# Attention in a two-layer diffusion backbone: the value products of two heads issued key block by key block in turns

## The chip, the cores and the metric

The kernel runs on one core of a Trainium2 chip. The metric is device time in microseconds (us) of one execution. A core has TensorE (PE, with its weight loads shown as PEld), VectorE (DVE), ScalarE (ACT), GpSimd (POOL), SyncE (SP) and 16 DMA engines. Each engine works through its own instructions in a fixed order and waits on semaphores for the others.

## The reference, cut to what matters

Two layers are computed over 512 latent tokens and 256 context tokens of 1024 features. Each layer projects its input, runs four token mixers (multi-head latent attention, an RWKV-7 scan, grouped-query attention, windowed grouped-query attention), merges them with gates, applies an output projection and a norm, then a product-key expert network and a second norm. The change touches the three attentions. Each has 8 heads with values of 64 features. For a block of 128 queries of one head:

```python
s = einsum('bqkgd,blkd->bkgql', q, k) * scale     # scores of 128 queries against n keys
p = softmax(s)                                     # a sink logit joins in windowed attention
o = einsum('bkgql,blkd->bqkgd', p, v)              # values weighted: n keys x 64 features
```

A latent query sees all 768 keys in the first two attentions, so 6 key blocks of 128. In windowed attention it sees 512 or 640 keys (4 or 5 blocks). A context query sees the 256 context keys (2 blocks). The last layer has no context queries.

## The kernel before, in words

Layer 0 and layer 1 go through the same stages: projections, RWKV scan, attention and merge, output projection and norm, experts, second norm. In the attention stage `branch` (line 1104) is called three times, for latent (L1203), grouped-query and windowed attention (both L1227). It goes over the head pairs `hp`, over the streams (latent and context), over the 128-query blocks `b` and over the two heads of the pair. For each of these it calls `attend` (line 1061), which

- multiplies queries and keys into the scores `S`, a PSUM tile called `pw` with two buffers (L1070; masks L1073),
- takes the row maximum on VectorE (L1075) and its scaled negative (L1077, with a sink L1079),
- takes the exponential with its row sum on ScalarE into `pp`, three buffers (L1081),
- takes the reciprocal (L1085) and normalises the row (L1086), both on VectorE,
- transposes `pp` block by block on TensorE (L182) into PSUM tiles `ptp`, four blocks to a tile, two buffers; a tile of four blocks is copied to `pt` by ScalarE (L1097), a shorter one by VectorE (L1095),
- multiplies the values by `pt`, one matmul for each key block, accumulated in the PSUM tile `po` (L1101). The stationary operand is 128 keys x 64 features, the moving one 128 keys x 128 queries. The first head of the pair writes partitions 0 to 63 of `po`, the second 64 to 127. `po` has one buffer; when all query blocks of a stream are done it is split into two parts by ScalarE and VectorE (L1127, L1128).

Operands of the value products are float32, and the trace has two records of MATMUL and two of LDWEIGHTS for each such product.

`merge` (line 1034) multiplies a finished branch by its output weights (matmuls into `pm`, L176), with two VectorE operations for each piece (L1049, L1051) and a split of each weight tile (L204, L205). The merge of the branch before is written behind each branch and runs in between the matmuls of the next one.

The attention stage has no order written out by hand. When the program is built, a planner of the framework puts each engine's instructions in a fixed order: it goes through its own estimate of the run, and whenever an engine is free it takes the ready instruction that was written first. So work written later fills in where earlier work isn't ready by its estimate, and the chip then follows that order whatever the true times are.

The lines that decide on the value products are these:

```python
kbs = [k0 // P + j for c0, k0, kn in ranges for j in range(kn // P)]
r0 = (h % 2) * 64
for j, kb in enumerate(kbs):
    pe.matmul(o[r0:r0 + 64, o0:o0 + P], vx(kb), pt[:, j * P:(j + 1) * P],
              start=(j == 0), stop=(j == nk - 1))
```

Of the kernel before, what the change touches and what calls it, by code (L numbers as in the profile page):

```python
# [8 lines left out]
F32 = mybir.dt.float32  # L9
# [9 lines left out]
P = 128  # L19
D = 1024  # L20
DC = 8
TL = 512
TC = 256
T = TL + TC
# [54 lines left out]
def tile_backbone(ctx: ExitStack, tc: tile.TileContext, I, out, taps=None, upto=99):  # L79
# [89 lines left out]
    def mm_acc(outs, lhs, rhs, nk):  # L169
        """outs: list of (psum ap, lo, hi); lhs/rhs: functions k -> (H, L); moving sliced by lo:hi"""  # L170
# [13 lines left out]
    # ------------------------------------------------------------------ weight stream  # L184
# [26 lines left out]
    # ------------------------------------------------------------------ modulation  # L211
# [3 lines left out]
    def ada_round(l, r, ps, sb, ring=None, bufs=4):  # L215
        """columns r * 2048 .. of layer l: four groups of 512, one column tile of the array each"""
# [30 lines left out]
    def xtiles(l):  # L247
        """the modulated input of layer l in two parts, latent and context, on the other side of SBUF"""
# [7 lines left out]
    # ------------------------------------------------------------------ layers  # L256
    for l in range(DEPTH):
# [5 lines left out]
        with xlat:  # L263
            # ---------------------------------------------------------- S1 projections
            T3B = 12
            with xctx, ExitStack() as e1:
# [42 lines left out]
                # RWKV features, transposed  # L309
                with ExitStack() as er:  # L310
# [76 lines left out]
                    def prepare(hp, r, k, v, kk, rt):  # L387
                        """decayed queries and keys of a pair of heads, bonus"""
# [95 lines left out]
                # natural projections  # L484
# [22 lines left out]
                def rope(dst, x, b, nh, hd):  # L507
                    """dst, x: [P, nh, hd]"""
# [80 lines left out]
                # context gates  # L589
# [36 lines left out]
            # ---------------------------------------------------------- S2 RWKV scan, latent gates  # L626
            ybscr = dram.tile([P, 4, T], F32, name=f"ybscr{l}")
            with ExitStack() as e2:
# [29 lines left out]
                class Halves:  # L658
                    """twelve chunks in two tiles: forward in the order of the steps, backward by chunk"""
# [9 lines left out]
                    def load(self, rows, src, first):  # L669
                        """src(a, b): chunks a .. b - 1"""  # L670
# [22 lines left out]
                def rwkv_pair(hp, loaded, others):  # L693
                    """others: what is left to do for the pair before, done between the parts of this one; yields
                    when only the norm is left"""
# [5 lines left out]
                    # Gram blocks  # L701
# [13 lines left out]
                    # inverse of the 32 x 32 diagonal blocks  # L715
# [7 lines left out]
                    # strictly causal part of the values, per step  # L723
# [59 lines left out]
                    # chunk recurrence  # L783
# [91 lines left out]
                    # group norm, bonus, gate  # L875
# [69 lines left out]
        def fold(pool, go, bo, m, kshift, kscale):  # L945
            """gain and bias of the norm, then scale and shift of the modulation, as one gain and one bias"""
# [8 lines left out]
        def layer_norm(pool, psv, pm, z, lo, hi, go, bo, dst, GB=None, dests=None, nat=None):  # L955
            """tokens lo..hi of z: [P, DC, TN], normalised in place over the features; pm: its column sums;
            dst: where the result goes; dests(lo, hi, s): where its modulated form goes, in two parts"""
# [57 lines left out]
        with ExitStack() as ep:  # L1015
# [7 lines left out]
            # -------------------------------------------------------------- S3 attention and merge  # L1023
            with ExitStack() as e3:
# [36 lines left out]
                def attend(pool, q, kx, vx, scale, h, o, o0, ranges, masks, sink):  # L1061
                    """one 128-query block of one head; ranges: (S column, first key, keys)"""
# [24 lines left out]
                    pt = pool.tile([P, T], F32, name=nm("pt"), tag="pt", bufs=3)  # L1087
# [10 lines left out]
                    kbs = [k0 // P + j for c0, k0, kn in ranges for j in range(kn // P)]  # L1098
                    r0 = (h % 2) * 64
                    for j, kb in enumerate(kbs):  # L1100
                        pe.matmul(o[r0:r0 + 64, o0:o0 + P], vx(kb), pt[:, j * P:(j + 1) * P],  # L1101
                                  start=(j == 0), stop=(j == nk - 1))
# [143 lines left out]
            with ExitStack() as eh:  # L1246
# [67 lines left out]
                def spend(e, c):  # L1314
                    """engine e is busy for c more"""
                    clock[e] = max(clock[e], clock["pe"] - SLACK[l]) + c
# [664 lines left out]
```

## Time and profile before

| what | value |
|---|---|
| time, median of 3 runs | 6534.53 us (6518.1 to 6548.82) |
| span of the profiled execution | 6533.5 us |
| PE busy | 5912.4 us (90%) |
| PEld busy | 4895.5 us (75%) |
| DVE busy | 4508.9 us (69%) |
| ACT busy | 2371.0 us (36%) |
| POOL busy | 2217.2 us (34%) |
| value products (L1101) in the chain that ended last | 4% of the span |

The span goes from the first to the last instruction of the profiled execution. Its own time isn't listed apart from the three timed runs; the span is 1.0 us under their median. Busy time is what an engine's records cover. Matmuls are pipelined and the ends of their records are modelled, so a row's time is longer than the step from one matmul to the next. "idle before it" is time in which an engine stood still ahead of an instruction, with the instruction whose end let it go.

### The profile page before, as it was taken

What the parts mean: (1) busy time and instruction counts of PE and PEld (TensorE: products, weight loads), DVE (VectorE), ACT (ScalarE), POOL (GpSimd) and SP (SyncE); (2) the same over time, 40 slices, a digit from 0 to 9 for tenths busy, and PEclk for the clock granted to TensorE, in tenths of its full rate; (3) what the DMA queues carried; (4) which work ended last, traced back from release to release, by engine and by line L of the source; (5) the groups of instructions that cost most, each with busy time, mean ns of one, the idle gap of its engine ahead of it and who ended that gap; (6) DMA issues with size and microseconds to landing.
All of it is one profiled execution on the core that took longest, in us unless ns stands there. A gap on an engine that the chain in (4) does not pass through costs nothing.

```text
span 6533.5 us, 95628 instructions
## 1 busy us (share of the span) xinstructions
PE 5912.4 (90%) x35605; PEld 4895.5 (75%) x35605; DVE 4508.9 (69%) x9402; ACT 2371.0 (36%) x4585; POOL 2217.2 (34%) x1721
## 2 busy tenths in 40 slices
PE   8898998999897998889899788798999888999998
PEld 5677665778776886667677566666678788999998
DVE  6535554667698857888888674546456798578887
ACT  3223222444335842222222332222334467433333
POOL 1101222000038846656655211133100168444442
PEclk9998897999998999999999899799899999999999
DMA  4455222031435688888899435422121446888896
GB/s 175 157 192 181 84 85 72 11 87 58 148 109 185 229 280 305 303 305 315 316 334 335 171 107 177 131 93 74 68 64 41 156 148 226 291 292 294 296 331 246
DMA packets 532162, 1220.90 MB, mean 187 GB/s; under 512 B 46321, under 2 KB 249201, under 8 KB 524017
## 3 DMA queue, kind: packets, MB, share of 16 engines
q1 hardware_dynamic: 339728, 718.16, 33.2%
q0 software_dynamic: 111168, 406.63, 17.0%
q10 hardware_dynamic: 80800, 90.00, 4.0%
q8 instruction: 281, 4.60, 0.3%
q14 instruction: 185, 1.51, 0.1%
HBM read 1041.41 MB, written 173.21 MB: 186 GB/s over the span
## 4 chain that ended last, share of the span: by engine, by line
PE 48%; DVE 14%; issue 8%; DMA 8%; POOL 5%; ACT 2%; SPq 0%; ACTq 0%; POOLq 0%; DVEq 0%
PE pu L1538 10%; PE pa L1789 7%; PE po L1101 4%; POOL row L1008 3%; PE pl L176 3%; PE pm L176 3%; DMA row<-in_peer_v,gix 3%; PE pw L1070 3%; PE ptp L182 2%; PE pv L1789 2%; PE pn L499 2%; DMA row<-in_peer_v 2%; PE pg L1465 2%; DMA row<-in_peer_u,gix 2%; PE pw L176 1%
## 5 line engine op out<-in xcount | busy, mean ns | idle before, releaser
L1538 PE MATMUL pu<-HX,wH 128*128 128x512 f32 (+2 forms) x4608 | 1327.4, 371 | 11.5 <-ACT wH L1524 6.0
L1538 PEld LDWEIGHTS pu<-HX,wH 128*128 128x128 f32 x4608 | 855.9, 194 | 115.1 <-ACT ga L1777 7.0
L1538 PE MATMUL pu<-HX,wL 128*128 128x512 f32 (+2 forms) x2304 | 848.3, 368 | 41.6 <-POOL wL L1526 36.1
L1008 POOL DMA_INDIRECT row<-in_peer_u,gix x384 | 495.3, 1290 | 513.9 <-DVE row L1648 281.1
L1008 POOL DMA_INDIRECT row<-in_peer_v,gix x384 | 495.5, 1290 | 454.6 <-DVE accn L1657 237.9
L1630 ACT CAST wH<-row 128x1024 fp32r<-128x1024 f32 x384 | 401.9, 1047 | 609.2 <-DMA row<-in_peer_v 286.6
L1789 PE MATMUL pa<-CL,wH 128*128 128x512 f32 (+1 forms) x1536 | 566.5, 369 | 26.0 <-DVE CL L1769 25.8
L1789 PE MATMUL pa<-CH,wH 128*128 128x512 f32 (+1 forms) x1536 | 563.7, 367 | 21.5 <-ACT CH L1764 21.4
L1648 DVE SCALAR_TENSOR_TENSOR row<-row,hn 128x1024 f32<-128x1024 f32 x384 | 504.4, 1323 | 99.0 <-DMA row<-in_peer_u,gix 96.8
L1789 PE MATMUL pa<-CH,wL 128*128 128x512 f32 (+1 forms) x1536 | 562.3, 366 | 0.0
L1657 DVE SCALAR_TENSOR_TENSOR accn<-row,gcw,accn 128x1024 f32<-128x1024 f32 x381 | 519.3, 1374 | 61.4 <-DMA row<-in_peer_v,gix 60.8
L1646 DVE TENSOR_TENSOR wL<-row,wH 128x1024 fp32r<-128x1024 f32 x384 | 478.3, 1246 | 119.4 <-ACT wH L1630 118.6
L1538 PEld LDWEIGHTS pu<-HX,wL 128*128 128x128 f32 x2304 | 445.4, 193 | 100.9 <-POOL wL L1526 42.7
L204 ACT CAST wH<-wr 128x1024 fp32r<-128x1024 f32 (+1 forms) x222 | 231.0, 1043 | 574.9 <-PE pl L176 188.4
L980 POOL TENSOR_TENSOR lnst<-lnst,mhalf 128x4 f32<-128x4 f32 (+3 forms) x8 | 9.4, 1180 | 1183.1 <-DVE lnst L979 1183.1
L176 PE MATMUL pl<-X,wH 128*128 128x512 f32 x1024 | 403.7, 457 | 3.7 <-DVE qk L585 3.2
L205 POOL TENSOR_TENSOR wL<-wr,wH 128x1024 fp32r<-128x1024 f32 x64 | 214.4, 3355 | 545.4 <-ACT wH L204 278.2
L1449 POOL TENSOR_SCALAR B<-cst,T 128x128 f32<-128x128 f32 x330 | 383.4, 1170 | 33.6 <-PE pg L1465 20.7
L1789 PEld LDWEIGHTS pa<-CL,wH 128*128 128x128 f32 x1536 | 291.2, 190 | 72.2 <-DVE CL L1769 41.3
L1789 PEld LDWEIGHTS pa<-CH,wH 128*128 128x128 f32 x1536 | 291.2, 190 | 61.4 <-ACT CH L1764 29.1
L205 DVE TENSOR_TENSOR wL<-wr,wH 128x1024 fp32r<-128x1024 f32 (+1 forms) x158 | 191.3, 1213 | 189.3 <-ACT wH L204 188.1
L1764 ACT CAST CH<-ga 128x512 fp32r<-128x512 f32 (+1 forms) x256 | 145.0, 566 | 467.6 <-DVE ga L1761 349.3
(400 smaller groups left out, 13619.4 us busy)
## 6 DMA issues: line engine op xcount, KB each, us to landing
row<-in_peer_v SPq DMA_DIRECT2D x256, 512.0 KB
wr<-in_uT SPq DMA_DIRECT2D x128, 512.0 KB
row<-in_uT SPq DMA_DIRECT2D x128, 512.0 KB
wr<-in_ada_w SPq DMA_DIRECT2D x96, 512.0 KB
wr<-in_w_gate SPq DMA_DIRECT2D x96, 512.0 KB
gdr<-gall SPq DMA_DIRECT2D x32, 1024.0 KB
Gt<-gdr SPq DMA_DIRECT2D x32, 1024.0 KB
gdr<-big SPq DMA_DIRECT2D x24, 1024.0 KB
```

The source lines that it names most:

```text
L176: pe.matmul(o, lw, rw[:, lo:hi], start=(k == 0 and a == 0), stop=(k == nk - 1 and a == 2))
L204: ac.copy(H, raw)
L205: lsplit[0] = (split or ve).tensor_tensor(L, raw, H.bitcast(F32), op=OP.subtract)
L1008: gp.indirect_dma_start(out=rows, out_offset=None, in_=tab, in_offset=bass.IndirectOffsetOnAxis(ap=ix, axis=0))
L1101: pe.matmul(o[r0:r0 + 64, o0:o0 + P], vx(kb), pt[:, j * P:(j + 1) * P], start=(j == 0), stop=(j == nk - 1))
L1449: (gp if e == "gp" else ve).tensor_scalar(B[:, j, :], iota, T3[:, 1, t_ + j:t_ + j + 1], T3[:, 2, t_ + j:t_ + j + 1], op0=OP.is_equal, op1 ...
L1538: pe.matmul(pw[:, :hi - lo], w[:, k, :], x[:, k, :], start=(k == 0 and i == 0), stop=(k == DC - 1 and i == 2))
L1630: ac.copy(H, ready[nx[1]])
L1646: ve.tensor_tensor(L, raw, H.bitcast(F32), op=OP.subtract)
L1648: ve.scalar_tensor_tensor(raw, raw, 1.0, hn[y], op0=OP.mult, op1=OP.mult, accum_out=acts[y][:, j:j + 1])
L1657: ve.scalar_tensor_tensor(accn[y], raw, gcw[y][:, j:j + 1], accn[y], op0=OP.mult, op1=OP.add)
L1789: pe.matmul(pv[:, :TD], w[:, ds], x, start=(k == 0 and i == 0 and (fresh or s == 0)), stop=(k == 1 and i == 2 and (fresh or s == NS - 1)))
```

## The change

`attend` no longer issues the value products: it returns the tile `pt` and the list of key blocks. `branch` calls it for both heads of the pair and then calls a new function, `weighted`, which goes over the key blocks and issues for each the product of the first head and that of the second. The number of products, their shapes, operands and outputs stay as they were. `pt` gets a fourth buffer (3,072 bytes more of each partition). The rest of the diff takes out comments.

```diff
-                def attend(pool, q, kx, vx, scale, h, o, o0, ranges, masks, sink):
+                def attend(pool, q, kx, scale, ranges, masks, sink):
...
-                    pt = pool.tile([P, T], F32, name=nm("pt"), tag="pt", bufs=3)
+                    pt = pool.tile([P, T], F32, name=nm("pt"), tag="pt", bufs=4)
...
-                    kbs = [k0 // P + j for c0, k0, kn in ranges for j in range(kn // P)]
-                    r0 = (h % 2) * 64
-                    for j, kb in enumerate(kbs):
-                        pe.matmul(o[r0:r0 + 64, o0:o0 + P], vx(kb), pt[:, j * P:(j + 1) * P],
-                                  start=(j == 0), stop=(j == nk - 1))
+                    return pt, [k0 // P + j for c0, k0, kn in ranges for j in range(kn // P)]
+
+                def weighted(o, o0, vs, found):
+
+                    nk = len(found[0][1])
+                    for j in range(nk):
+                        for i, (pt, kbs) in enumerate(found):
+                            pe.matmul(o[i * 64:i * 64 + 64, o0:o0 + P], vs[i](kbs[j]), pt[:, j * P:(j + 1) * P],
+                                      start=(j == 0), stop=(j == nk - 1))
...
                             for b in range(lo // P, hi // P):
+                                found = []
                                 for h in (2 * hp, 2 * hp + 1):
...
-                                    attend(pool, qp(h, b), kget(h), vget(h), scale, h, o, b * P - lo, rg, masks,
-                                           None if sinks is None else sinks[:, h:h + 1])
+                                    found.append(attend(pool, qp(h, b), kget(h), scale, rg, masks,
+                                                        None if sinks is None else sinks[:, h:h + 1]))
+                                weighted(o, b * P - lo, [vget(h) for h in (2 * hp, 2 * hp + 1)], found)
```

## Rows read from the trace of the kernel before

**Rows 1.** The page: busy engines, and the chain that ended last.
```profile
PE 5912.4 (90%) x35605; PEld 4895.5 (75%) x35605; DVE 4508.9 (69%) x9402; ACT 2371.0 (36%) x4585; POOL 2217.2 (34%) x1721
...
PE pu L1538 10%; PE pa L1789 7%; PE po L1101 4%; POOL row L1008 3%; PE pl L176 3%; PE pm L176 3%; DMA row<-in_peer_v,gix 3%; PE pw L1070 3%; PE ptp L182 2%; PE pv L1789 2%; PE pn L499 2%; DMA row<-in_peer_v 2%; PE pg L1465 2%; DMA row<-in_peer_u,gix 2%; PE pw L176 1%
```

**Rows 2.** Windows: six attention stretches and a gap; columns in their first line.
```profile
core 0: us, PE busy (x) PEld busy (x) DVE busy (x) ACT busy (x) POOL busy (x), PEclk, DMA share, GB/s
1166.00:1305.00 139.00, 137.88 (x867) 101.15 (x866) 91.33 (x243) 59.97 (x132) 0.00 (x0) 1.00 0.05 13
1336.00:1490.00 154.00, 150.56 (x1024) 123.21 (x1022) 107.33 (x284) 67.27 (x145) 0.00 (x0) 1.00 0.25 68
1498.00:1616.00 118.00, 114.98 (x816) 96.60 (x814) 86.63 (x283) 61.76 (x172) 0.00 (x0) 1.00 0.14 41
4716.00:4831.00 115.00, 114.83 (x711) 83.54 (x709) 70.72 (x159) 49.98 (x96) 0.00 (x0) 1.00 0.04 11
4859.00:4983.00 124.00, 122.85 (x811) 97.69 (x810) 81.67 (x184) 56.11 (x107) 0.00 (x0) 1.00 0.21 59
4991.00:5076.00 85.00, 81.93 (x589) 67.67 (x587) 55.45 (x166) 46.42 (x117) 0.00 (x0) 1.00 0.10 29
4830.00:4890.00 60.00, 52.40 (x285) 40.23 (x283) 30.59 (x64) 20.21 (x36) 0.00 (x0) 0.94 0.56 153
```

**Rows 3.** Line 1101: records, ns min/median/max, first and last start; idle time before them.
```profile
L1101 PEld LDWEIGHTS po<-pt,vg x1472: 132/137/231, 1336.4 to 5075.7; 128*64 128x64 f32 x184
L1101 PE MATMUL po<-pt,vg x1472: 272/273/476, 1336.4 to 5075.8; 128*64 128x128 f32 x184
...
L1101 PE MATMUL po<-pt,vm x832: 272/273/324, 1166.5 to 4830.8; 128*64 128x128 f32 x167
...
  ACT pt L1097: 62.3, 154
```

**Rows 4.** Timeline, value products: start, us, engine, line, operation, count.
```profile
1402.22 0.65 PE L1101 MATMUL po<-pt,vg 128*64 128x128 f32 x4
...
1231.48 0.66 PE L1101 MATMUL po<-pt,vm 128*64 128x128 f32 x8
...
1231.47 0.42 PEld L1101 LDWEIGHTS po<-pt,vm 128*64 128x64 f32 x8 [0.29 <-PE pw L1070]
...
1514.64 1.58 PE L1101 MATMUL po<-pt,vg 128*64 128x128 f32 x16
```

**Rows 5.** Timeline, latent attention of layer 0, two heads in a row.
```profile
1253.91 0.88 PE L182 MATMUL ptp<-cst,pp 128*128 128x128 f32 x6
1253.99 0.62 DVE L1086 TENSOR_SCALAR pp<-pp,mx 128x768 f32<-128x768 f32 x1
1254.62 1.03 PE L1070 MATMUL pw<-kT,qT 96*128 96x256 f32 x4
1254.66 0.59 ACT L1097 COPY pt<-ptp 128x512 f32<-128x512 f32 x1 [0.90 <-PE ptp L182]
...
1255.58 1.28 PEld L1101 LDWEIGHTS po<-pt,vm 128*64 128x64 f32 x12 [0.33 <-ACT pt L1097]
1255.58 1.52 PE L1101 MATMUL po<-pt,vm 128*64 128x128 f32 x12
1257.03 0.64 PEld L182 LDWEIGHTS ptp<-cst,pp 128*128 128x128 f32 x6 [0.17 <-issue]
```

**Rows 6.** Groups by line: count, busy us, mean ns, idle time before them.
```profile
L1075 DVE TENSOR_REDUCE mx<-pw 128x1 f32<-128x768 f32 x128 | 121.9, 954 | 26.3 <-PE pw L1070 25.6
L1081 ACT ACTIVATE pp<-pw,mx 128x768 f32<-128x768 f32 x128 | 115.5, 902 | 101.3 <-DVE mx L1077 97.0 <-PE pw L1070 1.6 <-DVE mx L1085 1.0
L1097 ACT COPY pt<-ptp 128x512 f32<-128x512 f32 x192 | 112.3, 586 | 189.9 <-PE ptp L182 188.1 <-PE pw L1070 1.0
L1086 DVE TENSOR_SCALAR pp<-pp,mx 128x768 f32<-128x768 f32 x128 | 79.1, 618 | 2.2
...
L1085 DVE RECIPROCAL mx<-mx 128x1 f32<-128x1 f32 x240 | 37.8, 158 | 28.7 <-ACT pp L1081 27.4
```

## The prediction, as it was put on record before the run

> **What bounds the kernel now.** I read the page first: TensorE is busy 90% of the span, VectorE 69%, and the value products are the third line of the chain that ended last, with 4% of 6,533.5 us, or 261 us [rows 1]. A share of a chain doesn't say what a change there is worth, so I read the busy times of the six stretches in which the three attentions of both layers run [rows 2]. They add up to 735 us. TensorE is busy 723 us of them (98%) at a granted clock of 1.00, VectorE 493 us (67%), ScalarE 342 us (46%), and DMA moves little. So TensorE ends last in this stage, and every microsecond taken from its queue comes off the span until another engine, or a wait between engines, ends last instead. The reader is to see in rows 2 both numbers at once: the full engine, and the next fullest one that will limit the gain.
>
> **What a value product costs.** The line has 1,472 and 832 matmul records, 2,304 in all, two for each product [rows 3]. One head's run of 12 records (six key blocks) takes 1.52 us [rows 5] and one of 4 records 0.65 us [rows 4], so a step is (1.52 - 0.65) / 8 = 0.109 us. The 0.65 us hold three steps (0.33), the last record's 0.273 us [rows 3] and 0.05 us extra at the start of a run. All products take 2,304 x 0.109 = 251 us of TensorE, and 240 runs (120 pairs of a query block, two heads each) another 12 us.
>
> **What taking turns gives.** The trace of before already holds the case that decides. With two key blocks a head makes 4 records, so the run of 8 at 1231.48 us is both heads of a pair, one right behind the other. It takes 0.66 us, where 4 records of one head take 0.65 us [rows 4]. Two heads whose products lie in different halves of the columns thus run side by side, in the time of one. The run of 16 at 1514.64 us is two heads with four blocks each, all four of one ahead of all four of the other. In a row they would take 0.65 + 12 x 0.109 = 1.96 us, side by side 0.65 + 4 x 0.109 = 1.09 us; the row shows 1.58 us. So with four products of one head in front less than half of the overlap comes, and the order in turns is what would give all of it. I found 18 such unbroken runs in the timeline, ten like the first (0.43 us saved each) and eight like the second (0.38 us): about 7 us of the overlap is had already. Everywhere else the two heads' products are apart, as in rows 5, where transposes follow a head's 12 records at once.
>
> If all 1,152 products of first and second heads ran in pairs, half of 251 us would go: 125.6 us, less those 7: **118 us of TensorE time**, 1.8% of the span. That is the far end.
>
> The Trainium skill, "TensorE: Matmul & The Clock Gate", section "Part 3: Packing small matmuls — row/col tiling", says that a weight load overlaps matmuls in flight only when its row group differs. Both heads here use all 128 rows, so by that rule the alternating loads would stand in the open, nothing would be freed and the time would stay at 6,534 us. The trace disagrees: in the run of 8 the eight loads take 0.42 us together, not eight times the 0.137 us of one [rows 3, 4].
>
> **What takes its place.** Each part of the change, with its cost:
>
> - *Products, transposes, copies:* as many as before and of the same shapes. The first head's products move behind the second head's scores, softmax, transposes and copies. No DMA is issued by the moved lines, and the queues of SP and POOL aren't passed.
> - *Cover that is lost.* The first head's 1.52 us of products now lie between its own copy and the second head's transposes. There they hid the second head's normalising: in rows 5 the VectorE row of 0.62 us at 1253.99 us ends 2.4 us ahead of the transposes at 1257.03 us that follow the products. That slack is more than the 1.36 us by which the transposes move forward, so in the steady state the transposes of the second head are ready. In exchange they now cover ScalarE's copy of the first head (0.59 us), for which TensorE stands still 0.33 us today [rows 5], and 62.3 us over 154 times in all [rows 3]. A pair would wait once, not twice: between 0 and -31 us. I take 0, since the planner may put the first head's first product ahead by itself, and then the wait stays with it.
> - *A lone first product.* It depends on the first head alone. If it goes ahead, one product in a pair's first head finds no partner: 120 x 0.218 = 26 us of the 118 are lost, and 120 more starts at 0.05 us are 6 us. Below nothing this can't go; the far side is 32 us. I count it within the sum below. The Trainium skill, "TensorEngine Tiling (Array Packing)", section "Tiling Modes", says that a change of tiling mode drains the array. [...]
> - *The wait at the block's head.* Twelve products now stand behind one wait for the second head's copy. Behind them in TensorE's queue are the next scores, for which VectorE waits. That is the slower rival.
> - *The fourth buffer of `pt`* keeps the next pair's copies from waiting on this block. It moves no data; 0 us, unless a later pool has to wait for the memory, of which no row shows an instance.
> - *VectorE.* It has 493 us of work here and keeps all of it. If the stage shrank by 118 us to 617 us, VectorE would be at 80% there. The highest share that it reaches in any of the six stretches is 86.63 of 118 us, 73% [rows 2]. If it couldn't get above that, the stage would end at 493 / 0.734 = 672 us: 63 us saved. A head's VectorE and ScalarE work is a chain (0.95 maximum, 0.90 exponential, 0.16 reciprocal, 0.62 normalising [rows 6]), and with little fill-in work left it is waits of this chain, not VectorE's sum, that hold the last part back.
> - *Clock.* The stretch from 4830 to 4890 us has TensorE at 87% and a granted clock of 0.94 [rows 2]. If the stage fell to that share it would run at 0.94, and 6% of 617 us is 37 us given back. I take 0 and keep 37 for the range.
>
> The two ends are 63 us (VectorE no fuller than it has been) and 118 us (TensorE stays full). I take **75 us**, near the first, because that is the nearest row and the lone product pulls the same way.
>
> **The sum.** 6,533.5 - 75 = 6,458.5 us of span. The span is 1.0 us under the median of the runs, so the median would be 6,459 us, 1.2% less.
>
> **The rivals.**
>
> 1. *TensorE stays the bound.* The turns are complete, waits are shared by a pair, and fill-in work from the merges covers the rest: 118 us, 6,416 us; with half of the waits gone as well, 31 us less. For it: 98% against 67%, and the slack of 2.4 us. Against it: VectorE would have to run at 80%. Chance 0.17.
> 2. *It doesn't do what it says.* The planner fixes the order. The first head's `pt` is ready about one head's period (3.12 us from transposes to transposes in rows 5) ahead of the second's, and a planner that takes whatever is ready would issue the first head's products at once, as before. Against it: both heads write one PSUM tile, and I take it that writes to one such tile stay in their written order. Then only the first product can go ahead. Time 6,534 us. The rule of the skill on weight loads would give the same. Chance 0.15.
> 3. *Slower: the queue behind the block.* TensorE stands at the block for the second head's copy, with the next pair's scores behind it, so VectorE starts from nothing for each pair. Then a pair costs scores 1.03, two maxima 1.91, exponential 0.90, reciprocal 0.16, normalising 0.62, transposes 0.88, copy 0.59, a wait of 0.33 and the block 1.52: 7.9 us [rows 5, 6], against 2 x 3.12 = 6.24 us now. For 96 latent pairs that is 1.7 x 96 = 162 us more, 6,697 us; half of the pairs so and half at the forecast's gain, about 6,578 us. It decides where the added idle time ahead of a block is over 1.31 us, the time that a pair of six blocks saves. For it: `pw` has only two buffers, so scores can't run far ahead. Against it: the slack of 2.4 us, and scores that today already stand between transposes and products. Chance 0.08.
>
> **How the numbers follow.** The forecast case has 0.60, its own range 6,425 to 6,502 us: the lower end is 108 us saved, the upper one the 75 us less the 37 us of clock, with a few us for the spread of the runs. What a measurement here can tell from no change is about 0.5%, 33 us, so faster means under 6,502 and slower over 6,567 us. Faster: 0.58 of the forecast and rival 1's 0.17, 0.75. Same: rival 2 and the forecast's tail, 0.17. Slower: 0.08. The range runs from 6,400 us (rival 1 with half of its shared waits) to 6,545 us (rival 2 and the spread of the runs) and leaves out most of rival 3.
>
> **What the profile of the changed kernel would show.** The products' step: runs of 24 records of both heads taking about 1.5 us, in place of 12; runs of 12 in 1.5 us followed by another such run would be rival 2. In the attention stretches TensorE's busy share would fall below 98% and VectorE's rise above 70%. The six stretches together would last about 660 us, not 735. VectorE's busy total and the instruction counts of this line would stay. If idle time ahead of the block grew by over 1.31 us for each pair, with VectorE waiting on the scores, rival 3 would be right. The forecast is wrong if the stage is as long as before, or if it shrinks and a later stage takes the time back.

## The result, and the profile after

The changed kernel takes 6443.92 us, median of four runs (6431.72 to 6454.95), beside 6541.67 us (6518.1 to 6554.73, four runs: the three of the table ahead and one more) of the kernel before on the same chip. The ratio is 0.985, with an interval from 0.9825 to 0.9875: 98 us less, between 82 and 114. The forecast was 6,459 us, 75 us less. The profiled execution after has a span of 6429.8 us, 103.7 us under that of before.

The page first: the engines' busy time, and the chain that ended last.

```profile
PE 5798.9 (90%) x35605; PEld 4788.5 (74%) x35605; DVE 4503.3 (70%) x9402; ACT 2367.3 (37%) x4585; POOL 2210.1 (34%) x1721
...
PE pu L1545 7%; PE pa L1796 6%; PE pl L176 2%; PE pv L1796 2%; PE pw L1071 1%; PE pm L176 1%; PE po L1106 1%; PE ptp L182 1%; DVE B L1456 1%; PE pw L176 1%; PE pg L1472 1%; DVE X L745 1%; DVE tmp L742 1%; PE pw L807 0%; PE pw L809 0%
```

Against rows 1, every engine has the same count of instructions and, but for TensorE, nearly the same busy time. TensorE's matmuls are busy 113.5 us less and its weight loads 107.0 us less. The value products (now L1106) fall from 4% of the chain to 1%.

The groups of that line, in the kernel before and after. The columns are: count, then busy us and mean ns of one, then the idle time of the engine before them.

```profile
L1101 PE MATMUL po<-pt,vg 128*64 128x128 f32 x1472 | 194.6, 279 | 6.2 <-ACT pt L1097 3.5 <-DVE mx L1084 0.3
...
L1101 PE MATMUL po<-pt,vm 128*64 128x128 f32 x832 | 104.2, 277 | 0.8 <-DVE mx L1077 0.4 <-ACT pt L1097 0.3
```

```profile
L1106 PE MATMUL po<-pt,vg 128*64 128x128 f32 x1472 | 131.7, 281 | 2.1 <-ACT pt L1098 1.1 <-DVE YL L1135 0.2
...
L1106 PE MATMUL po<-pt,vm 128*64 128x128 f32 x832 | 70.4, 280 | 0.0
```

The same 2,304 records, each as long as before (some 0.28 us), cover 202.1 us instead of 298.8, because they lie side by side. That is 96.7 us.

The six attention stretches after, in the order of rows 2 and with its columns:

```profile
1158.00:1279.00 121.00, 119.19 (x855) 82.89 (x852) 88.94 (x240) 59.41 (x131) 0.00 (x0) 1.00 0.04 12
1311.00:1460.00 149.00, 145.95 (x1126) 118.13 (x1125) 118.37 (x311) 72.71 (x160) 0.00 (x0) 1.00 0.30 81
1460.00:1560.00 100.00, 93.68 (x745) 75.02 (x742) 79.09 (x268) 58.59 (x166) 0.00 (x0) 1.00 0.12 35
4658.00:4755.00 97.00, 96.95 (x707) 67.01 (x706) 68.87 (x157) 48.85 (x96) 0.00 (x0) 1.00 0.05 13
4782.00:4882.00 100.00, 96.94 (x767) 74.52 (x767) 76.04 (x173) 52.27 (x100) 0.00 (x0) 0.99 0.27 70
4888.00:4972.00 84.00, 81.87 (x652) 65.45 (x651) 62.59 (x183) 50.24 (x126) 0.00 (x0) 1.00 0.15 45
```

They add up to 651 us against 735 in rows 2; with the gaps between grouped-query and windowed attention (8 and 8 us before, none and 6 after) to 657 against 751, so 94 us less. TensorE is busy 634.6 of the 651 us, 97%: it still ends last. VectorE has the same 494 us as before, now 76% of the stage. The granted clock stays at 0.99 to 1.00.

Timeline of TensorE after, latent attention of layer 0, a little over one pair of heads:

```profile
1253.30 1.52 PE L1106 MATMUL po<-pt,vm 128*64 128x128 f32 x22
1254.76 0.87 PE L182 MATMUL ptp<-cst,pp 128*128 128x128 f32 x6
1255.46 1.46 PE L1071 MATMUL pw<-kT,qT 96*128 96x256 f32 x4
1256.76 0.82 PE L182 MATMUL ptp<-cst,pp 128*128 128x128 f32 x6
1257.51 0.43 PE L1106 MATMUL po<-pt,vm 128*64 128x128 f32 x2
1257.87 0.70 PE L1071 MATMUL pw<-kT,qT 96*128 96x256 f32 x2
...
1259.54 1.52 PE L1106 MATMUL po<-pt,vm 128*64 128x128 f32 x22
```

The first head's first product goes ahead alone (2 records, 0.43 us; the next matmul starts 0.36 us after the start of this one). Runs of two like it stand in 115 places of the trace, for 120 pairs. The other eleven products of the pair, 22 records, take 1.52 us: as long as the 12 records of one head in rows 5. The weight loads run side by side too; they and the waits for ScalarE's copies, in the same trace:

```profile
1253.30 1.28 PEld L1106 LDWEIGHTS po<-pt,vm 128*64 128x64 f32 x22 [0.76 <-ACT pt L1098]
...
1257.51 0.19 PEld L1106 LDWEIGHTS po<-pt,vm 128*64 128x64 f32 x2 [0.17 <-issue]
```

```profile
L1106 PE MATMUL po<-pt,vg x1472: 272/273/476, 1311.3 to 4971.8; 128*64 128x128 f32 x184
...
L1106 PE MATMUL po<-pt,vm x832: 272/273/324, 1158.2 to 4754.3; 128*64 128x128 f32 x167
...
  ACT pt L1098: 37.9, 99
```

22 loads take 1.28 us, as 12 did in rows 5. The wait for ScalarE's copies is 37.9 us over 99 times, against 62.3 over 154 in rows 3; nearly all of both is time of the weight loads' queue (36.8 and 58.5 us), the rest of the matmuls'.

### The profile page after: what moved, and what is told of

Read it like the earlier page. It is cut to its first block, busy times and chain, and to the rows that moved or that the text cites. A ratio compares the mean times of both kernels' runs of the same rounds, so it can differ in the third digit from the quotient of the medians.

```text
span 6429.8 us, 95669 instructions
## 1 busy us (share of the span) xinstructions
PE 5798.9 (90%) x35605; PEld 4788.5 (74%) x35605; DVE 4503.3 (70%) x9402; ACT 2367.3 (37%) x4585; POOL 2210.1 (34%) x1721
## 5 line engine op out<-in xcount | busy, mean ns | idle before, releaser
L1796 PEld LDWEIGHTS pa<-CH,wH 128*128 128x128 f32 x1536 | 291.8, 190 | 62.3 <-ACT CH L1771 30.4
L1796 PEld LDWEIGHTS pa<-CH,wL 128*128 128x128 f32 x1536 | 291.8, 190 | 30.6
```

What stands on the lines that cost most here:

```text
L1796: pe.matmul(pv[:, :TD], w[:, ds], x, start=(k == 0 and i == 0 and (fresh or s == 0)), stop=(k == 1 and i == 2 and (fresh or s == NS - 1)))
```

## The experiments

The theory after the result: the gain comes from products of both column halves standing close together in TensorE's queue, and nothing else in the stage matters much. The rivals: the new order of the heads does it without any overlap; VectorE or a wait for it limits what comes out; the memory of the fourth buffer or the waits for the copies play a part.

The edits are shown against the changed kernel, except where said. In the table, "line" is the busy time of the value products' matmul records. "Stage" is the time from the first to the last of these records, added over four stretches (latent attention; grouped-query and windowed attention together; both layers). "Wait" is the wait of these products, weight loads and matmuls, for ScalarE's copies. All are from one profiled execution each; the ratio is from the timed runs, to the kernel before on the same chip. That kernel took 6533 us on the chip of the first four experiments, 6541 on that of the next four and 6537 on that of the turns, so ratios are compared, not times.

| kernel | time, us | ratio (95%) | line | stage | wait |
|---|---|---|---|---|---|
| before | 6541.67 | 1 | 298.8 | 748.1 | 62.3 |
| changed | 6443.92 | 0.985 (0.9825 to 0.9875) | 202.1 | 654.3 | 37.9 |
| one half of the columns | 6525.81 | 0.9975 (0.9947 to 1.0003) | 273.9 | 735.5 | 40.7 |
| head by head | 6547.94 | 1.0019 (1.0005 to 1.0033) | 301.2 | 755.0 | 56.5 |
| second head first | 6398.63 | 0.9762 (0.9732 to 0.9793) | 152.6 | 603.9 | 37.4 |
| half of the products | 6443.74 | 0.9848 (0.9821 to 0.9875) | 181.8 | 662.9 | 72.7 |
| three buffers | 6457.01 | 0.9868 (0.9826 to 0.991) | 202.4 | 657.8 | 39.9 |
| one head later | 6423.62 | 0.9823 (0.9779 to 0.9866) | 160.2 | 617.0 | 36.7 |
| copies on ScalarE | 6391.27 | 0.9777 (0.9738 to 0.9816) | 152.5 | 591.5 | 43.6 |
| more for VectorE | 6464.67 | 0.9886 (0.9847 to 0.9924) | 202.7 | 665.6 | 35.9 |
| turns of two | 6383.30 | 0.9773 (0.9738 to 0.9808) | 157.7 | 607.7 | 36.6 |
| turns of three | 6415.36 | 0.9819 (0.9786 to 0.9853) | 178.9 | 626.4 | 37.5 |

Outside of the stage the profiled executions differ whatever the kernel: the span less the stage is 5785 us before, 5776 after, 5814 with the second head first and 5767 with turns of two. So where a few ten us matter, the stage and the line are read, and the ratio for the end to end.

The stage has two weaknesses of its own. The matmuls of the merges (`pm`) fill in there, and how many of them do differs: in the four stretches they are busy 153 us before, 150 in the changed kernel, 150 with the second head first, but 174 with half of the products, 141 with the copies on ScalarE and 138 with more for VectorE. And the granted clock, 1.00 in nearly all of the stage, fell to the lower of its levels (1.2 GHz) for more than 4 us in three of the profiled executions: 0.52 from 1224 to 1238 us with half of the products; 0.72 from 1499 to 1505 and 0.60 from 1555 to 1559 us with three buffers; 0.72, 0.72 and 0.66 in three stretches of 5 to 6 us with more for VectorE. Where TensorE is the bound these cost up to 7, 3 and 5 us, an estimate from the share of the clock that is missing.

**One half of the columns.** The changed order stays, but nearly all products of both heads go to one half of the columns.

```diff
                     for j in range(nk):
                         for i, (pt, kbs) in enumerate(found):
-                            pe.matmul(o[i * 64:i * 64 + 64, o0:o0 + P], ...,
-                                      start=(j == 0), stop=(j == nk - 1))
+                            end = i == 1 and j == nk - 1
+                            r0 = 64 if end else 0
+                            pe.matmul(o[r0:r0 + 64, o0:o0 + P], ...,
+                                      start=end or (i == 0 and j == 0), stop=end or (i == 0 and j == nk - 1))
```

> The changed kernel with the same order of instructions, but both heads' value products accumulate in the lower column half (partitions 0 to 63 of po); only the last product of the second head goes to the upper half, so the attention output isn't that of the reference. Nothing else is different: as many products, loads, copies. Theory (the gain is that two heads in different column halves run side by side): the products take 0.109 us a record again, one after the other, about 118 us of TensorE time come back, and the time is 6,530 to 6,580 us; runs of 22 records take about 2.6 us. Rival (the gain is the new order: one wait for copies per pair in place of two, better cover): the time stays at 6,444 us within 15.

The ratio is 0.9975 with 1 inside its interval; the time is 4 us under the theory's range. The runs of a pair, in TensorE's timeline:

```profile
1247.62 2.40 PE L1108 MATMUL po<-pt,vm 128*64 128x128 f32 x22
...
1252.27 0.43 PE L1108 MATMUL po<-pt,vm 128*64 128x128 f32 x2
1253.26 2.40 PE L1108 MATMUL po<-pt,vm 128*64 128x128 f32 x22
```

22 records in a row would take 0.65 + 18 x 0.109 = 2.61 us; the row shows 2.40 us, 0.21 us less, because the last product of the second head still goes to the other half. That is one product of 0.218 us for each of 120 pairs, 26 us, and the line is 25 us less busy than before. The other 72 us of the changed kernel's gain in this line are gone. So the overlap of the two heads' products is the gain; what little is left here (the stage is 13 us shorter than before, the ratio's interval reaches 1) is no more than that last product gives.

In this kernel both heads also write to one place of PSUM, so it doesn't tell the column half from the place. The trace of before does. In the RWKV scan, line 857 has four products of 128x64, with 64 moving columns, that go to both halves and to two places in each. In its runs of 8 records the records start in twos, 7 ns apart, and the third and fourth two each start 59 ns behind the one ahead. By the order of the code the third begins the second place of each half, and a new place alone gains it nothing.

**Head by head.** Both heads are normalised first, as in the changed kernel, but all products of the first head go ahead of all of the second.

```diff
-                    for j in range(nk):
-                        for i, (pt, kbs) in enumerate(found):
+                    for i, (pt, kbs) in enumerate(found):
+                        for j in range(nk):
```

> Both heads of a pair are normalised first, as in the changed kernel, with four buffers of pt, but then all products of the first head are written ahead of all of the second. Theory: the planner issues the first head's products as soon as its copies are there, so the heads are apart in TensorE's queue again and little overlaps: 6,500 to 6,545 us, and the timeline shows runs of 12 records in 1.5 us. Rival (the move behind both heads gives the gain, the turns don't): 6,444 us within 15.

The ratio is 1.0019, the line 301.2 us busy: the turns are needed. (The time is 3 us over the theory's range.) The planner sends the first head's products ahead where they are ready (runs of 12), and where both heads' products do stand together they overlap at one place only:

```profile
1243.51 1.52 PE L1106 MATMUL po<-pt,vm 128*64 128x128 f32 x12
1247.17 1.52 PE L1106 MATMUL po<-pt,vm 128*64 128x128 f32 x12
...
1257.64 2.45 PE L1106 MATMUL po<-pt,vm 128*64 128x128 f32 x24
```

In a row 24 records would take 0.65 + 20 x 0.109 = 2.83 us. The one change of half saves 0.38 us, as much as in the run of 16 of rows 4 (0.38 us as well).

**Second head first.** In each turn the second head's product is issued ahead of the first head's, so that no product of the block is ready before both heads are.

```diff
-                        for i, (pt, kbs) in enumerate(found):
+                        for i in (1, 0):
+                            pt, kbs = found[i]
```

> As the changed kernel, but in each turn the second head's product comes ahead of the first head's. The changed kernel's timeline shows one product of the first head (2 records) going ahead alone and 22 records following; with the second head in front no product can go ahead alone, all 24 records stand together. Theory (the lone product costs 0.218 us of TensorE a pair and about 0.2 us around it): up to 20 us faster than the changed kernel, 6,424 to 6,444 us. Rival (the lone product fills a gap in which TensorE would wait anyway for the second head's copy): the same as the changed kernel or slower, 6,444 to 6,460 us.

This is faster than the changed kernel by more than was expected, and under both ranges: its interval, 0.9732 to 0.9793, ends below that of the changed kernel, and the stage is 50 us shorter. The line's groups, two runs of the timeline, and the stage in four stretches (columns as in rows 2):

```profile
L1107 PE MATMUL po<-pt,vg 128*64 128x128 f32 x1472 | 98.3, 278 | 3.1 <-ACT pt L1098 1.7 <-DVE pt L1096 0.9
...
L1107 PE MATMUL po<-pt,vm 128*64 128x128 f32 x832 | 54.3, 277 | 0.2 <-DVE pt L1096 0.2
```

```profile
1251.13 1.53 PE L1107 MATMUL po<-pt,vm 128*64 128x128 f32 x24
...
1256.84 1.53 PE L1107 MATMUL po<-pt,vm 128*64 128x128 f32 x24
```

```profile
1178.00:1293.00 115.00, 113.81 (x869) 80.94 (x870) 87.73 (x240) 57.27 (x128) 0.00 (x0) 1.00 0.07 21
1327.00:1554.00 227.00, 214.83 (x1831) 180.47 (x1831) 191.48 (x571) 126.16 (x318) 0.00 (x0) 0.99 0.25 67
4667.00:4760.00 93.00, 92.64 (x712) 65.06 (x713) 68.03 (x154) 47.62 (x93) 0.00 (x0) 1.00 0.05 16
4789.00:4959.00 170.00, 166.07 (x1428) 134.60 (x1429) 142.71 (x362) 104.18 (x230) 0.00 (x0) 1.00 0.21 62
```

The lone product is gone: a pair is one run of 24 records in 1.53 us. The line is 49.5 us less busy than in the changed kernel, 0.41 us for each of the 120 pairs, which is the length of the lone run (0.43 us). The stage is 605 us here; TensorE is still 97% busy in it (587 us) and VectorE 81% (490 us), 84% in the second stretch. So neither 73% nor 76% of VectorE was a limit.

**Half of the products.** The kernel before, with every other key block's product left out.

```diff
-                    for j, kb in enumerate(kbs):
...
+                    some = [j for j in range(nk) if j % 2 or nk == 5 and (h % 2 == 0 and j == 4)]
+                    for j in some:
...
```

> The kernel before, head after head, with half of the value products left out (576 of 1,152 are issued: every second key block), so the attention output isn't that of the reference. TensorE's time for products is that of perfect pairs, without the need to have both heads ready. Theory (part of the 118 us is not had because VectorE and the chain of waits end last, whoever issues the products): 6,430 to 6,450 us, as the changed kernel. Rival (the part that is missing is lost by waiting for both heads): 6,410 to 6,425 us.

It comes out at the changed kernel's time (0.9848 against 0.985). That equality would fit a stage that ends by VectorE in both. But the kernel with the second head first goes well under this time with all of VectorE's work in it, so VectorE doesn't end it here. The line, and then its wait, show what happens:

```profile
L1102 PE MATMUL po<-pt,vg 128*64 128x128 f32 x736 | 118.7, 286 | 7.7 <-ACT pt L1097 4.1 <-DVE YL L1129 0.4 <-DVE mx L1077 0.3
...
L1102 PE MATMUL po<-pt,vm 128*64 128x128 f32 x416 | 63.1, 285 | 0.9 <-ACT pt L1097 0.8
```

```profile
  ACT pt L1097: 72.7, 176
```

The line is 117 us less busy than before, the stage only 85 us shorter. Of the 32 us between them, TensorE's other records take 21: matmuls of the merges moved into the stage (174 us busy against 153), and some records are longer at the lower clock. (Before it fell, TensorE was busy 5.9 of 7 us, and then waited 1.14 us for ScalarE.) Added idle time takes the other 11 us, from 12 to 23; the wait for the copies is up by 10 us. So this kernel's time doesn't price the changed kernel's overlap, and its equal time is a coincidence. Its line stays 29 us above that of the second head first, though both need TensorE for as many steps: leaving out products of a head's run leaves the two runs of a pair and their starts and ends in place, and merging the runs takes those away too.

**Three buffers.** `pt` with the three buffers of before.

```diff
-                    pt = pool.tile([P, T], F32, name=nm("pt"), tag="pt", bufs=4)
+                    pt = pool.tile([P, T], F32, name=nm("pt"), tag="pt", bufs=3)
```

> The changed kernel with three buffers of pt, as before, in place of four. A pair holds two of them until its block of products is done, so the second head of the next pair has no buffer for its copies while the block waits. Theory (the fourth buffer keeps the copies of the next pair off this wait): a part of the gain is lost, 6,455 to 6,500 us. Rival (the buffer does nothing, the turns alone count): 6,444 us within 15.

The time of 6457 us lies in both ranges. The ratio is 0.9868 (0.9826 to 0.991), the line and the wait are those of the changed kernel, and the stage is 3.5 us longer, which is about what the lower clock in two places of it costs. An effect of the buffer under some 10 us can't be told from none here, and the stage shows no larger one.

**One head later.** On top of the second head first, the block is written after the next pair's first head, so that the copies have more time.

```diff
+                            late = None
...
                                     found.append(attend(...))
-                                weighted(o, b * P - lo, [vget(h) for h in (2 * hp, 2 * hp + 1)], found)
+                                    if late is not None:
+                                        weighted(*late)
+                                        late = None
+                                late = (o, b * P - lo, [vget(h) for h in (2 * hp, 2 * hp + 1)], found)
+                            weighted(*late)
```

> The variant with the second head in front (6,399 us), and each pair's block of products is written one head later, behind the first head of the next query block of the same stream, so that the planner has the next scores and transposes ahead of it. Theory (what is left to gain is TensorE's wait for ScalarE's copy ahead of each block, 37.4 us over 92 times in that variant): the wait mostly goes, 6,365 to 6,390 us. Rival (the planner fills there already, or the next head's transposes come to wait in its place): 6,399 us within 12, or slower.

The wait stays (36.7 us against 37.4), the line is 7.6 us busier and the stage 13 us longer than with the second head first. The theory that more distance takes this wait away fails; what the wait costs, a run in which it stays can't tell. By the trace TensorE's idle time of all kinds is 18 us in the stage of the kernel with the second head first (605 - 587), so it can't be more than that. The timeline shows that the wait is still there ahead of some blocks, and that others are now cut in two:

```profile
1246.65 1.53 PE L1107 MATMUL po<-pt,vm 128*64 128x128 f32 x24 [0.74 <-ACT pt L1098]
1253.73 0.88 PE L1107 MATMUL po<-pt,vm 128*64 128x128 f32 x12
1255.34 0.88 PE L1107 MATMUL po<-pt,vm 128*64 128x128 f32 x12
```

**Copies on ScalarE.** On top of the second head first, ScalarE makes all copies of `ptp` to `pt`, and VectorE none.

```diff
-                        if m < 4:
+                        if m < 4 and False:
```

> The variant with the second head in front, with all copies of transposes on ScalarE: VectorE loses 208 copies of 0.42 us (74 us and more of its work in the stage), ScalarE gets them. Theory (TensorE and its waits for ScalarE's copies end last, not VectorE): no gain, 6,395 to 6,430 us, as the two copies of a head now stand one behind the other on ScalarE. Rival (VectorE ends last): 6,360 to 6,385 us.

The two longest of the four stretches:

```profile
1315.00:1534.00 219.00, 212.03 (x1815) 175.31 (x1814) 167.69 (x488) 145.61 (x397) 0.00 (x0) 1.00 0.24 64
...
4750.00:4922.00 172.00, 167.94 (x1431) 134.95 (x1430) 130.27 (x317) 113.83 (x278) 0.00 (x0) 1.00 0.21 61
```

VectorE's busy time in the four stretches falls by 62 us, from 490 to 428 (the 208 copies have 83 us of records, which overlap others), and the stage becomes 12 us shorter (591.5 against 603.9); TensorE's line is the same. Of the 12 us, 9 are matmuls of the merges that no longer fall into the stage (141 against 150 us). The time, 6391 us, lies between the two ranges, and the ratio, 0.9777, can't be told from 0.9762. So less VectorE work is worth a fifth of its own time in the stage at most, and nothing that the end to end shows.

**More for VectorE.** The changed kernel with one more reduction on VectorE for each head and query block.

```diff
+                    more = pool.tile([P, 1], F32, name=nm("more"), tag="more", bufs=2)
+                    ve.tensor_reduce(more, pp[:, :n // 4], axis=AX.X, op=OP.max)
                     return pt, [k0 // P + j for c0, k0, kn in ranges for j in range(kn // P)]
```

> The changed kernel with one more VectorE operation for each head, a row maximum over a quarter of the normalised row, whose result nobody reads: 0.2 to 0.35 us each, about 70 us of VectorE in the stage. Theory (VectorE isn't what ends last in the changed kernel): the time goes up by less than 25 us, 6,440 to 6,468 us. Rival, which the forecast rested on (VectorE and its chain limit the gain): most of the 70 us come on top, 6,485 to 6,515 us.

The added group (line, form and the other forms; busy us), and the two longest of the four stretches:

```profile
L1100 DVE TENSOR_REDUCE more<-pp 128x1 f32<-128x192 f32 (+3 forms) x240 | 73.1, 306 | 2.0
```

```profile
1330.00:1589.00 259.00, 242.68 (x1859) 195.35 (x1858) 215.16 (x676) 131.05 (x324) 0.00 (x0) 0.99 0.22 60
...
4797.00:4990.00 193.00, 181.51 (x1426) 141.37 (x1425) 153.41 (x428) 107.47 (x233) 0.00 (x0) 0.99 0.21 58
```

The added records are 73 us long, but they overlap others: VectorE's busy time in the four stretches rises by 45 us, from 499 to 544. The stage becomes 11 us longer (665.6 against 654.3), with 12 us less of the merges' matmuls in it; so on equal work it is some 23 us, of which 4 go to the lower clock. The ratios differ by as much (0.9886 and 0.985, 24 us), but their intervals overlap. VectorE is at 83% and 79% in these stretches and TensorE at 94%. The theory's bound of 25 us holds, narrowly: had VectorE ended the stage, all of the 45 us would have come out, and by this count about half did.

**Turns of two and of three.** The second head first, with turns of two or three key blocks instead of one.

```diff
-                    for j in range(nk):
-                        for i in (1, 0):
+                    for j, i in [(j, i) for j0 in range(0, nk, 2) for i in (1, 0) for j in range(j0, min(nk, j0 + 2))]:
+                            pt, kbs = found[i]
```

> The kernel of the experiment that begins each turn with the second head, with turns of two key blocks instead of one: two products of the second head, then two of the first. Theory (the column halves work side by side wherever products of both halves stand close in the queue; in the kernel before two products of each half, four records and four, still overlapped in full, x8 records in 0.66 us): turns of two cost nothing against turns of one, one time each near 6,399 us, 6,385 to 6,415; a run of a pair still takes about 1.53 us for 24 records, and the line's busy time stays near 153 us. Rival (only the next product in the queue can run beside the one at work, so each second product of a turn waits for its own half): half of the overlap is lost, the line's busy time goes up by some 70 us and the time to about 6,470 us.

> The same with turns of three key blocks (pairs of five blocks end with a turn of two). Theory (the queue reaches a few products ahead, and the kernel before showed four products of a half and four of the other, eight records each, overlapping only in part): a part of the overlap is lost with three, the line's busy time at 165 to 215 us against 153 with turns of one, and the time 6,405 to 6,450 us. Rival (the reach is far longer than a turn of three): 6,399 us within 12 us, busy time near 153 us.

A run of a pair with six key blocks, and the line's groups, with turns of two and then of three:

```profile
1251.60 1.58 PE L1106 MATMUL po<-pt,vm 128*64 128x128 f32 x24
```

```profile
L1106 PE MATMUL po<-pt,vg 128*64 128x128 f32 x1472 | 101.8, 280 | 2.7 <-ACT pt L1098 1.3 <-DVE pt L1096 0.7
...
L1106 PE MATMUL po<-pt,vm 128*64 128x128 f32 x832 | 55.9, 279 | 0.2 <-DVE pt L1096 0.2
```

```profile
1250.75 1.80 PE L1106 MATMUL po<-pt,vm 128*64 128x128 f32 x24
```

```profile
L1106 PE MATMUL po<-pt,vg 128*64 128x128 f32 x1472 | 115.8, 278 | 3.2 <-ACT pt L1098 1.7 <-DVE pt L1096 0.9
...
L1106 PE MATMUL po<-pt,vm 128*64 128x128 f32 x832 | 63.1, 278 | 0.2 <-DVE pt L1096 0.2
```

Both theories hold (the time with turns of two is 2 us under its range): 24 records take 1.53 us with turns of one, 1.58 with two, 1.80 with three, and 2.45 where the heads follow one another whole. Turns of two end at the ratio of turns of one (0.9773 and 0.9762); turns of three are at 0.9819, and their stage is 22 us longer than with turns of one. The rival that only the next product in the queue can run beside the one at work is out, and so is a reach much longer than three.

## Why the prediction was right, and where its size was off

**TensorE bounds the stage, and what leaves its queue leaves the span: right.** The line lost 96.7 us, the stage 94 and the kernel 98 (82 to 114). The same holds for the second head first: 146 us in the line, 144 in the stage, and a ratio that means 135 to 175 us (0.0207 and 0.0268 of 6533). TensorE is 96 to 98% busy in the stage of every kernel here, the one with more work for VectorE among them (96%).

**Products of two heads run side by side when issued in turns: right.** The run of 8 in rows 4 was the case that decided, and 22 records in 1.52 us are what it foretold. (The overlap had already was nearer 6 us than 7: of the 18 unbroken runs, the twelve of 8 records save 0.17 to 0.42 us each and the six of 16 records 0.19 to 0.39.) The rule on weight loads in the Trainium skill ("TensorE: Matmul & The Clock Gate", "Part 3: Packing small matmuls — row/col tiling") doesn't describe this: both heads use all 128 rows, and 22 loads took 1.28 us, as long as 12 did [rows 5].

**The lone first product: foreseen, and cost nearly as priced against the kernel before.** The planner sends exactly one product ahead. The text had 26 us for the lost partner and 6 us for 120 more starts. The starts aren't more: a pair had two runs before and has two now. With the 26 us alone the far end of 118 us becomes 92 us, 2 us from the stage's 94. What the text missed is on the other side. Were the lone product to go, a pair would have one run instead of two, and a run's start (0.05 us) and end (0.273 - 0.109 = 0.16 us) would go with it: 120 x 0.21 = 25 us. So what this idea could give was not 118 us but 143, counted by the records, whose ends are modelled; the second head first, at 146 us of the line and 144 of the stage, is there.

**Lost cover and waits, taken at 0 out of 0 to -31 us: right in size, from a number that meant less than it seemed.** The wait of rows 3 fell by 24 us as if pairs waited less often, but TensorE's idle time in the stage went from 12 us [rows 2] to 16 us (651 - 634.6). The 62.3 us is time in which the weight loads' queue stood still; most of it lies under matmul records that still run by the trace, and so it was never there to be saved. The kernel one head later was to save the wait that is left, which stayed, and its stage is 13 us longer.

**VectorE as the next limit: this is the term that was mis-sized.** The forecast took the highest share that VectorE had reached, 73%, as a limit near which the gain would end: 63 us, and so 75 for the sum. VectorE went to 76% of the stage in the changed kernel and to 81% with the second head first, while TensorE stayed at 97%. Taking 62 us of busy time from it gave 12 us of stage, 9 of them merge work that moved out; adding 45 us cost 11, or some 23 on equal work. So its work isn't free, but it didn't hold the gain back. The share that an engine has reached while another one ends last doesn't tell what it can reach. Without this term the text's own numbers, 118 - 26, give 92 us; the stage gave 94 and the runs 98. That 75 came as near as it did is in part luck: the 43 us taken off the 118, mostly for VectorE, stood where the lone product's 26 us belonged.

**The clock, 0 taken and 37 kept for the range: right at 0.** The granted clock is 0.99 or 1.00 in all six stretches. The stretch with the low clock in rows 2, from one attention to the next, was no pattern for the stage, and its share of 87% alone doesn't make 0.94: another gap between two attentions in the same trace shows 83% at 1.00 (columns as in rows 2).

```profile
1305.00:1336.00 31.00, 25.73 (x137) 22.86 (x136) 10.65 (x18) 3.82 (x6) 0.00 (x0) 1.00 0.76 204
```

The kernels in which the clock did fall within the stage lost up to 7 us by it, not 37.

**The fourth buffer at 0 us: not contradicted.** With three buffers the stage is within 3.5 us, and the clock accounts for those.

**The rivals.** That TensorE stays the bound (0.17) named the right mechanism and 118 us for it; with its lone product it would have been nearest. That the planner doesn't pair the products didn't happen, except in the kernel head by head, where it sent the first head's products ahead just as this rival described. The slower rival, a queue behind the block, needed 1.31 us of added idle time for each pair; the wait ahead of the products is 37.9 / 120 = 0.32 us for each pair, less than the 0.52 us before.

What stays open: whether shifts of some 10 us in the stage (copies on ScalarE, three buffers) come out at the end, and what VectorE's added work costs more exactly than 11 to 24 us. Both lie within what the rest of the span varies by.

## What to carry to other kernels

Look in the trace of before for a place where the thing you plan already happens by chance: one run of 8 records in the time of 4 priced this change better than any rule. When an order is made by a planner, write first what becomes ready last; turning two lines of a turn around was worth half as much again as the change itself. Don't read an engine's highest busy share so far as its limit: bound the gain by the work of the engine that ends last, and give the next engine a price only where a wait for it is seen. And when a stage is timed by its first and last record, look whether the same work lies between them.

## What the runs showed of the hardware that was not expected

In an unbroken run each change from one column half to the other saves nearly two products' time (2 x 0.218 us) at most. With 24 records of 0.65 + 20 x 0.109 = 2.83 us in a row, one change of half gives 0.38 us (2.45), three give 1.03 us (1.80, 0.34 each), five give 1.25 us (1.58) and eleven 1.30 us (1.53), where all of the overlap there is would be 12 x 0.109 = 1.31 us. So turns need to be no finer than two products of this size. Why the reach is that long was not tried.

A lone product of two records costs TensorE 0.43 us by its records and 0.36 us up to the next matmul, against 0.218 us for a product within a run, and against next to nothing for one with a partner in the other half (24 records of a pair take 1.53 us, 12 of one head 1.52).

A change between 64 and 128 stationary columns shows at both ends of a run. The first step of a run of products in one half, 128x64, is 0.160 us instead of 0.109. The first record of transposes, 128x128, takes 0.328 us right behind a run and 0.274 behind scores of 96x128, so that six records take 0.87 us there and 0.82 behind scores (the timeline after). The scores have another number of rows, and that change shows nothing.
